# First MLP: two quarters of the up-projection in seven block products each pair of tiles

## The chip, the core and the metric

The program runs on one core of a Trainium2 chip. The metric is the device time of the whole program in microseconds, the median of several executions. The engines in the rows below are TensorE (PE, with its weight loads as PEld), VectorE (DVE), ScalarE (ACT), GpSimd (POOL) and SyncE (SP), which issues the loads of weights.

## What is computed

Two transformer blocks over 512 tokens of width 1024, all in fp32. The first block has an attention mixer, a recurrence, and the MLP that the change is about. The second has two layers whose norms are modulated by `m`, a product of a vector with `ada_w`; the first layer also reads 256 context tokens.

```
hn = rmsnorm(h, norm2_g)
a = square(relu(hn @ w_ff1))        # 1024 -> 4096
h = h + a @ w_ff2                   # 4096 -> 1024
...
m_lat = silu(c) @ ada_w[i] + ada_b[i]       # 6 x 1024 columns for each of two layers
m_ctx = silu(c_ctx) @ ada_w[i] + ada_b[i]
h_lat = rmsnorm(x, g) * (1 + sc_m) + sh_m ; h_ctx = likewise from ctx
```

## The kernel before

Every fp32 operand is held as a pair, a rounded part `hi` and the rest `lo`, and each product of two 128-blocks is three matmuls (`mm3`, L181 to L190: hi.hi, hi.lo, lo.hi). Activations stand transposed, eight tiles of 128 x 512 tokens. A weight tile of 128 x 1024 comes in one load of 512 KB on SP's queue into one of three buffers `wr` (L154); ACT casts it to `wh` (L139), DVE subtracts to `wl` (L128), and 8 x 3 matmuls of 512 columns use the two. `wh` and `wl` have three buffers each. The scheduler fixes the order on each engine before the run; every engine takes its instructions in that order.

The columns of the modulation `m` are computed on DVE beside the MLPs: `ada` (L455) loads a 128 x 1024 tile into a `wr` buffer, the same three as the weights use (L462), and one DVE operation `adaj` multiplies it with silu(c) and sums it (L468). The first 16 columns of layer 0 are needed for the context too and are multiplied twice, with silu(c_ctx) from a second `silu` tile. The table `ADA[0]` says at which step of the first MLP each of the 48 columns is issued. A step is one up-projection tile or one down-projection tile: `tick` in `mlp` (L550) calls `extra` (L710), which looks the step up, and also takes the next piece of the context's work (`CTX`).

The first MLP (`mlp_one`, called at L730) takes the up-projection in four quarters of eight tiles (`ff1`) and the down-projection in four (`ff2`): ff1(0), ff1(1), ff2(0), ff1(2), ff2(1), ff1(3), ff2(2), and the last down-projection in `down` (L317). In all four quarters each tile is multiplied plainly: 24 matmuls of 512 columns.

The MLPs of the second block (`modulated_mlp`, L1108) already use another form. There, from the second quarter on, two weight tiles r0 and r1 are multiplied together, as a 2 x 2 block matrix, with seven products instead of eight (`seven`, L505): DVE forms four sums of weight blocks, seven factors are split, 84 matmuls of 256 columns follow, and DVE recombines the products into two result tiles. The sums of the activations that this needs are made once (`block_sums`, L480). Such groups (p0 to p3) stand between the down-projection columns of the quarter before (m0 to m7) by the lists `MIXED` (L52).

Of the kernel before, what the change touches and what calls it, by code (L numbers as in the profile page):

```python
# [19 lines left out]
F32R = mybir.dt.float32r  # L20
# [4 lines left out]
AF = mybir.ActivationFunctionType  # L25
ALU = mybir.AluOpType
# [4 lines left out]
TC = 256  # L31
# [13 lines left out]
"""  # L45
TAGS = dict(sb=6, hg=16, gate=7)
LATER = (15, 32, 14, 26, 7, 26, 8, 29, 8, 40, 10, 31, 14, 40, 5, 29)
ADA = ((2, 2, 3, 4, 5, 6, 8, 8, 9, 9, 10, 11, 12, 13, 14, 15, 18, 19, 20, 21, 22, 23, 25, 26, 27, 28, 29, 30, 31, 32, 33, 34, 36, 37, 38, 39, 40, 41, 42, 43, 44, 45, 46, 47, 48, 50, 51, 51), (9, 11, 13, 15, 17, 19, 21, 23, 25, 27, 29, 31, 33, 35, 37, 39, 41, 43, 45, 47, 49, 51, 53, 55))
# [31 lines left out]
MAN = ""  # L80
TAIL = "t0 t1 t2 p0 p1 p2 w3"
ENG = dict(scale="P", kr="DP", kp="DP", pt="D", v="D", k="D", cos="P")
CTX = (20, 22, 25, 26, 27, 28, 30)


class Kernel:
# [390 lines left out]

    def block_sums(self, xs, eng=None):  # L480


        B = [[] for _ in range(7)]
        a0, a1 = HALF
        add, sub = ALU.add, ALU.subtract

        def step(k):
            x, y = (self.S(name="bx") for _ in range(2))
            for z, (h, l) in ((x, xs[k]), (y, xs[k + 4])):
                self.tt(z, h.bitcast(F32), l.bitcast(F32), add, eng)  # L490
            out = [(self.F(TC, F32R, "bh", "cb"), self.F(TC, F32R, "bl", "cb")) for _ in range(3)]
            out.append(tuple(z[:, a1] for z in xs[k]))
            t, u = (self.S(name="bt") for _ in range(2))
            t1, t2, t3, t4 = t[:, a0], t[:, a1], u[:, a0], u[:, a1]
            for i, (d, p, q) in enumerate(((t1, x[:, a1], x[:, a0]), (t2, y[:, a1], t1), (t3, y[:, a1], x[:, a1]))):
                self.tt(d, p, q, sub, eng)
                self.split_into(*out[i], d)
            self.tt(t4, y[:, a0], t2, sub, eng)
            for i, b in enumerate((tuple(z[:, a0] for z in xs[k]), tuple(z[:, a0] for z in xs[k + 4]),
                                   tuple(z[:, a1] for z in xs[k + 4]), out[3], *out[:3])):  # L500
                B[i].append(b)
            return lambda: self.split_into(*out[3], t4)
        return B, step

    def seven(self, w, w_next, B, eng):  # L505

        nc = self.nc
        r0, r1 = self.wraw(w), self.wraw(w_next)
# [1 line left out]
        a11, a12, a21, a22 = r0[:, lo], r0[:, hi], r1[:, lo], r1[:, hi]  # L510
        add, sub = ALU.add, ALU.subtract
        a0, a1 = HALF
        s3, s1, s2, s4 = (self.S(name="ws") for _ in range(4))

        def pair(*parts):
            h, l = (self.wp.tile([128, 1024], F32R, tag=t, name=t) for t in ("wh", "wl"))
            for i, p in enumerate(parts):
                c = slice(512 * i, 512 * i + 512)
                self.split_into(h[:, c], l[:, c], p)
            return [self.wsplit((h[:, 512 * i:512 * i + 512], l[:, 512 * i:512 * i + 512]), 4) for i in range(len(parts))]  # L520
        self.tt(s3, a11, a21, sub, eng)
        self.tt(s1, a21, a22, add, eng)
        self.tt(s2, s1, a11, sub, eng)
        self.tt(s4, a12, s2, sub, eng)
        y, x = self.O(), self.P()
        w11, w3 = pair(a11, s3)
        w1, w2 = pair(s1, s2)
        w12, w22 = pair(a12, a22)
        w4, = pair(s4)
        p, s, v = self.H("p1"), self.S(name="p57"), self.H("u2")  # L530
        u = [self.S(name="u") for _ in range(2)]
        k = dict(skip_group_check=True)
        self.mm3(x[:, a0], w11, B[0], True, True)
        nc.scalar.copy(p, x[:, a0])
# [12 lines left out]
        self.tt(u[0][:, a1], y[:, a0], v, add)  # L547
        return u

    def mlp(self, w1, w2, xs, residual, scale=None, extra=None, down=None, begin=None, fast=None):  # L550


        step = [0]
# [43 lines left out]

        def ff1_fast(g, j, r):

            u = self.seven(w1[g * 8 + j], w1[g * 8 + j + 4], B, fast)  # L600
            for i in (1, 0):
                self.stt(u[i], u[i], 0.0, u[i], ALU.max, ALU.mult)
                r[j + 4 * i] = self.split(u[i], tag="f")
                tick()

        if fast:
            B, sums = self.block_sums(xs)
            late = []
            acts = ff1(0, lambda j: late.append(sums(j - 3)) if 3 <= j < 7 else None)
            for f in late:  # L610
                f()
            for g in range(3):
# [53 lines left out]
    def mlp_one(self):  # L666
# [949 lines left out]
```

## Time and profile before

| | us |
|---|---|
| median of 3 executions | 2096.09 |
| lowest and highest | 2095.75, 2098.06 |
| the profiled execution | 2098.49 |
| its span in the trace | 2096.8 |
| first MLP in the trace | 433 to 785 |
| attention of the second block, about | 790 to 1110 |
| second MLP, mixed quarters, about | 1190 to 1400 |

The trace is of one execution. Busy times are those of an engine's records; matmuls overlap one another, so their rate is read from the starts of neighbouring records, not from their lengths. In a row of a timeline the bracket at the end tells how long the engine was idle before it and which instruction ended that.

### The profile page before, as it was taken

Reading aid. Unit: us, or ns where it says so; the run is one execution under the profiler, and the core shown is the slowest. Engines: PE = TensorE matmul, PEld = TensorE weight load, DVE = VectorE, ACT = ScalarE, POOL = GpSimd, SP = SyncE. Lnnn points to the kernel's source line nnn. Section 1 sums busy time; section 2 is a strip of 40 time slices with the busy share of each in tenths; the row PEclk is TensorE's granted clock in tenths of the full one; section 3 lists DMA queues with packets and bytes.
Section 4 is the critical chain, followed back from the end, with each engine's and each line's share of the span. In section 5 each row is a group of like instructions: output and inputs, shape, how many; then the busy total and the mean of one; then the engine's idle time right before and its main releaser. Section 6 shows DMA issues by size and latency. Waiting matters only on the chain.

```text
span 2096.8 us, 29863 instructions
## 1 busy us (share of the span) xinstructions
PE 2057.1 (98%) x11414; PEld 1783.7 (85%) x11414; DVE 1506.5 (72%) x2860; ACT 929.2 (44%) x1600; POOL 218.2 (10%) x234
## 2 busy tenths in 40 slices
PE   9999999999999999899989999999999999999999
PEld 7888888887888888789878888988888889899897
DVE  6868775789766557888868787886457657777673
ACT  5546573444332324567655434443323334444341
POOL 0313220000100001345421000000000001000000
PEclk9999999999999999999999999999999999999999
DMA  5212121556666532101031344443325561232232
GB/s 174 71 61 66 46 85 51 156 180 199 187 186 191 170 121 87 34 22 36 31 121 60 126 155 143 141 161 120 101 89 182 162 192 58 84 109 101 91 111 91
DMA packets 73921, 238.84 MB, mean 114 GB/s; under 512 B 8241, under 2 KB 12593, under 8 KB 73778
## 3 DMA queue, kind: packets, MB, share of 16 engines
q1 hardware_dynamic: 73778, 236.94, 35.5%
q8 instruction: 89, 1.46, 0.3%
q14 instruction: 54, 0.44, 0.1%
HBM read 232.70 MB, written 4.20 MB: 113 GB/s over the span
## 4 chain that ended last, share of the span: by engine, by line
PE 81%; DVE 10%; DMA 3%; ACT 3%; issue 2%; POOL 0%; SPq 0%; POOLq 0%; ACTq 0%; DVEq 0%
PE pq L189 34%; PE ps L189 25%; PE po L189 11%; PE pg L189 2%; DVE wl L128 2%; DMA ada<-in_ada 2%; PE sc L220 1%; PE pl L220 1%; DMA wr<-in_ff 1%; DVE adaj L468 1%; DVE lo L128 1%; ACT wh L139 1%; DVE mod L131 1%; ACT pr L134 1%; PE o L189 1%
## 5 line engine op out<-in xcount | busy, mean ns | idle before, releaser
L139 ACT CAST wh<-wr 128x1024 fp32r<-128x1024 f32 (+3 forms) x362 | 324.8, 907 | 590.6 <-PE pq L189 259.7
L128 DVE TENSOR_TENSOR wl<-wr,wh 128x1024 fp32r<-128x1024 f32 (+3 forms) x362 | 378.4, 1052 | 83.5 <-ACT wh L139 79.7
L189 PE MATMUL pq<-hi,wl 128*128 128x512 f32 (+1 forms) x896 | 342.4, 383 | 0.4 <-DVE wl L128 0.4
L189 PE MATMUL pq<-hi,wh 128*128 128x512 f32 (+1 forms) x896 | 342.1, 383 | 0.0
L189 PE MATMUL pq<-lo,wh 128*128 128x512 f32 (+1 forms) x896 | 342.1, 383 | 0.0
L468 DVE SCALAR_TENSOR_TENSOR adaj<-ada,silu 128x1024 bf16<-128x1024 f32 x112 | 136.8, 1221 | 118.8 <-DMA ada<-in_ada 118.4
L189 PE MATMUL ps<-hi,wh 128*128 128x512 f32 x528 | 208.8, 396 | 2.0 <-ACT hi L139 1.2
L189 PE MATMUL ps<-hi,wl 128*128 128x512 f32 x528 | 209.0, 396 | 0.7 <-DVE wl L128 0.7
L189 PE MATMUL ps<-lo,wh 128*128 128x512 f32 x528 | 207.7, 394 | 0.0
L189 PEld LDWEIGHTS pq<-hi,wl 128*128 128x128 f32 x896 | 168.5, 188 | 33.5 <-DVE wl L128 1.1
L189 PEld LDWEIGHTS pq<-hi,wh 128*128 128x128 f32 x896 | 168.7, 188 | 32.4 <-issue 0.2
L189 PEld LDWEIGHTS pq<-lo,wh 128*128 128x128 f32 x896 | 168.6, 188 | 31.4
L189 PE MATMUL ps<-hl,wh 128*128 128x256 f32 (+1 forms) x752 | 180.3, 330 | 1.7 <-DVE m L128 0.9
L128 POOL TENSOR_TENSOR hl<-mod,hl 128x256 fp32r<-128x256 f32 x36 | 31.7, 890 | 1155.4 <-ACT hl L393 930.2
L189 PEld LDWEIGHTS ps<-hl,wh 128*128 128x128 f32 x752 | 128.0, 190 | 16.5 <-DVE u L128 2.0
L189 PE MATMUL ps<-hl,wl 128*128 128x256 f32 (+1 forms) x376 | 123.8, 329 | 0.0
L189 PEld LDWEIGHTS ps<-hi,wh 128*128 128x128 f32 x528 | 99.3, 188 | 23.7 <-ACT hi L139 1.4
L189 PEld LDWEIGHTS ps<-hi,wl 128*128 128x128 f32 x528 | 99.5, 188 | 22.7 <-DVE wl L128 1.6
L131 DVE SCALAR_TENSOR_TENSOR x<-pq,m,x 128x512 f32<-128x512 f32 (+1 forms) x88 | 60.4, 686 | 79.8 <-PE pq L189 79.7
L189 PEld LDWEIGHTS ps<-lo,wh 128*128 128x128 f32 x528 | 99.7, 189 | 20.0 <-DVE lo L128 0.4
L189 PE MATMUL po<-hl,wh 128*128 128x256 f32 (+1 forms) x528 | 115.4, 312 | 0.0
L139 ACT CAST wh<-ws 128x512 fp32r<-128x512 f32 x96 | 56.8, 619 | 96.1 <-PE po L189 66.7
(407 smaller groups left out, 4519.6 us busy)
## 6 DMA issues: line engine op xcount, KB each, us to landing
wr<-in_f SPq DMA_DIRECT2D x128, 512.0 KB, 3.5
ada<-in_ada SPq DMA_DIRECT2D x96, 512.0 KB, 3.9
wr<-in_ff SPq DMA_DIRECT2D x64, 512.0 KB, 4.2
wr<-in_w_in SPq DMA_DIRECT2D x41, 512.0 KB, 3.6
wr<-in_gw_v SPq DMA_DIRECT2D x16, 512.0 KB, 3.4
wr<-in_gw_u SPq DMA_DIRECT2D x16, 512.0 KB, 3.5
wr<-in_gw_o SPq DMA_DIRECT2D x16, 512.0 KB, 4.3
wr<-in_w_out SPq DMA_DIRECT2D x8, 512.0 KB, 3.7
```

The source lines that it names most:

```text
L128: return (eng or self.nc.vector).tensor_tensor(out=out, in0=a, in1=b, op=op)
L131: (eng or self.nc.vector).scalar_tensor_tensor(out=out, in0=a, scalar=s, in1=b, op0=op0, op1=op1)
L134: self.nc.scalar.activation(out=out, in_=x, func=func, scale=scale, bias=bias, **k)
L139: nc.scalar.copy(hi, x)
L189: self.nc.tensor.matmul(out, l, r, start=start and i == j == 0, stop=stop and i == n - 1 and j == 2, **k)
L220: self.nc.tensor.matmul(out, l, r, start=start, stop=stop)
L468: nc.vector.scalar_tensor_tensor(out=d, in0=w, scalar=1.0, in1=s, op0=ALU.mult, op1=ALU.mult, accum_out=m[:, n:n + 1])
```

## The change

The third and fourth quarter of the first MLP's up-projection go through `seven`, as in the MLPs of the second block. `mlp` gets two parameters. `plain=2` keeps quarters one and two plain; then the first down-projection runs, with `block_sums` issued behind its columns m4 to m7, and two mixed groups follow, by `MIXED[0]` and `MIXED[1]`. `tags` puts the 24 tiles of the sums into the buffers in which the context lay (`cx`, `xc`). The weight sums of a group go into a `silu` tile, two at a time, where s2 and s4 overwrite s3 and s1; the results go into `relu` tiles. Since this MLP scales its rows by rstd, DVE now forms relu times scale and ACT squares it.

The table of the modulation columns is new: the first 16 are issued at steps 2 to 14, none at steps 15 to 23, and the other 32 from step 24 to 54, one behind every step. The context's work goes from steps 20 to 30 to steps 8 to 20. In `seven` the sums and splits stand in another order, for all callers.

```diff
@@ tables
-ADA = ((2, 2, 3, 4, 5, 6, 8, 8, 9, 9, 10, 11, 12, 13, 14, 15, 18, 19, 20, 21, 22, 23, 25, 26, ...
+ADA = ((2, 2, 3, 3, 4, 5, 6, 7, 8, 8, 9, 10, 11, 12, 13, 14, 24, 24, 25, 26, 27, 28, 29, 30, ...
-CTX = (20, 22, 25, 26, 27, 28, 30)
+CTX = (8, 15, 16, 17, 18, 19, 20)
@@ block_sums
-            out = [(self.F(TC, F32R, "bh", "cb"), self.F(TC, F32R, "bl", "cb")) for _ in range(3)]
+            out = [tuple(self.F(TC, F32R, "b", next(tags) if tags else "cb") for _ in range(2)) for _ in range(3)]
...
-            t, u = (self.S(name="bt") for _ in range(2))
+            t, u = self.two(tags, "bt")
@@ new, called by block_sums and seven
+    def two(self, small, name):
+        if not small:
+            return [self.S(name=name) for _ in range(2)]
+        t = self.F(1024, name=name, tag="silu")
+        return t[:, :512], t[:, 512:]
@@ seven
-        s3, s1, s2, s4 = (self.S(name="ws") for _ in range(4))
...
+        s3, s1 = self.two(small, "ws")
+        s2, s4 = (s3, s1) if small else self.two(small, "ws")
...
         self.tt(s3, a11, a21, sub, eng)
         self.tt(s1, a21, a22, add, eng)
+        hl = pair()
+        w11, w3 = part(hl, 0, a11), part(hl, 1, s3)
         self.tt(s2, s1, a11, sub, eng)
+        hl = pair()
+        w1 = part(hl, 0, s1)
         self.tt(s4, a12, s2, sub, eng)
+        w2 = part(hl, 1, s2)
+        hl = pair()
+        w12, w22 = part(hl, 0, a12), part(hl, 1, a22)
+        w4 = part(pair(), 0, s4)
         y, x = self.O(), self.P()
-        w11, w3 = pair(a11, s3)
-        w1, w2 = pair(s1, s2)
-        w12, w22 = pair(a12, a22)
-        w4, = pair(s4)
         p, s, v = self.H("p1"), self.S(name="p57"), self.H("u2")
-        u = [self.S(name="u") for _ in range(2)]
+        u = [self.F(name="u", tag="relu") if small else self.S(name="u") for _ in range(2)]
@@ ff1_fast
             for i in (1, 0):
-                self.stt(u[i], u[i], 0.0, u[i], ALU.max, ALU.mult)
+                self.stt(u[i], u[i], 0.0, u[i] if scale is None else scale, ALU.max, ALU.mult)
+                if scale is not None:
+                    self.act(u[i], u[i], AF.Square)
                 r[j + 4 * i] = self.split(u[i], tag="f")
                 tick()
@@ mlp
-            B, sums = self.block_sums(xs)
+            B, sums = self.block_sums(xs, tags=tags)
             late = []
-            acts = ff1(0, lambda j: late.append(sums(j - 3)) if 3 <= j < 7 else None)
+            if plain == 1:
+                acts = ff1(0, lambda j: late.append(sums(j - 3)) if 3 <= j < 7 else None)
+            else:
+                acts = ff1(0)
+                nx = ff1(1)
+                for m in range(8):
+                    ff2(0, acts, (m,))
+                    if m >= 4:
+                        late.append(sums(m - 4))
+                acts = nx
             for f in late:
                 f()
-            for g in range(3):
+            for g in range(plain - 1, 3):
                 nx = [None] * 8
-                for what in (MIXED[0] if g == 0 else MIXED[1]).split():
+                for what in (MIXED[0] if g == plain - 1 else MIXED[1]).split():
@@ mlp_one
-        self.mlp(a["ff1"], a["ff2"], xs, residual, r2, extra, (self.Sum(self, gains=g2), done), begin=(2, start))
+        self.mlp(a["ff1"], a["ff2"], xs, residual, r2, extra, (self.Sum(self, gains=g2), done), (2, start),
+                 nc.vector, 2, iter(["cx"] * 8 + ["xc"] * 16))
```

`MIXED[0]` is "m0 m1 m2 p0 m3 p1 m4 p2 m5 p3 m6 m7", `MIXED[1]` is "m0 m1 p0 m2 p1 m3 m4 p2 m5 p3 m6 m7".

DVE, in the kernel before, third quarter: the first tile's relu (`relu`), its split (`lo`), a modulation column (`adaj` and its bias `m`), and the split of a later weight tile (`wl`).

```order
L131 SCALAR_TENSOR_TENSOR relu_6046<-ps_6021,rstd_4064 128x512 [waits PE_49]
L128 TENSOR_TENSOR wl_6147<-wr_6144,wh_6146 128x1024 [waits DMAHW2_49,Activation_49]
L468 SCALAR_TENSOR_TENSOR adaj_6227,m_79<-ada_6225,silu_4065 128x1024 [waits DMAHW5_49]
L128 TENSOR_TENSOR lo_6050<-relu_6046,hi_6049 128x512 [waits Activation_49]
L128 TENSOR_TENSOR m_79<-m_79,cols_72 128x1 [waits DVE_49]
L131 SCALAR_TENSOR_TENSOR relu_6089<-po_6064,rstd_4064 128x512 [waits PE_49]
```

DVE, in the changed kernel, where the first seven-product group of the third quarter begins: `h` takes up the result of the down-projection column m2, `b`, `bt` and `lo` belong to the block sums, `ws` are the weight sums, and `wl` 5571, 5578, 5585 and 5591 the splits of the group's factors.

```order
L128 TENSOR_TENSOR h_3813<-h_3813,pq_5532 128x512 [waits PE_49]
L128 TENSOR_TENSOR b_5423<-bt_5428,b_5422 128x256 [waits Activation_49]
L128 TENSOR_TENSOR bt_5428<-bx_5419,bt_5428 128x256 [waits DVE_49]
L128 TENSOR_TENSOR b_5425<-bt_5428,b_5424 128x256 [waits Activation_49]
L128 TENSOR_TENSOR b_5427<-bt_5428,b_5426 128x256 [waits Activation_49]
L128 TENSOR_TENSOR lo_3883<-bt_5428,hi_3882 128x256 [waits Activation_49]
L128 TENSOR_TENSOR ws_5567<-wr_5563,wr_5565 128x512 [waits DMAHW0_49,DVE_49]
L128 TENSOR_TENSOR ws_5567<-wr_5565 128x512
L128 TENSOR_TENSOR wl_5571<-ws_5567,wh_5570 128x512 [waits Activation_49]
L128 TENSOR_TENSOR wl_5578<-ws_5567,wh_5577 128x512 [waits Activation_49]
L128 TENSOR_TENSOR ws_5567<-ws_5567,wr_5563 128x512 [waits DVE_49]
L128 TENSOR_TENSOR wl_5585<-wr_5563,wh_5584 128x512 [waits Activation_49]
```

The weight sums and splits of the group stand behind the addition of m2's result and five operations of the block sums.

PE, in the kernel before, the same place: the first matmuls of the third quarter's first tile.

```order
L189 MATMUL ps_6021<-hi_3760,wh_6017 128x512 [waits Activation_49]
L189 MATMUL ps_6021<-lo_3761,wh_6017 128x512
L189 MATMUL ps_6021<-hi_3760,wl_6018 128x512 [waits DVE_49]
L189 MATMUL ps_6021<-hi_3800,wh_6017 128x512
L189 MATMUL ps_6021<-lo_3801,wh_6017 128x512
```

PE, in the changed kernel, first group of the third quarter: the last two matmuls of the first product (into `ps`, with the factor a11), and the beginning of the second (into `po`, whose factor is the weight sum s3).

```order
L189 MATMUL ps_5595<-lo_3883,wh_5570 128x256
L189 MATMUL ps_5595<-hi_3882,wl_5571 128x256
L189 MATMUL po_5594<-b_5267,wh_5570 128x256 [waits Activation_49]
L189 MATMUL po_5594<-b_5268,wh_5570 128x256
L189 MATMUL po_5594<-b_5267,wl_5571 128x256 [waits DVE_49]
L189 MATMUL po_5594<-b_5320,wh_5570 128x256
L189 MATMUL po_5594<-b_5321,wh_5570 128x256
```

The second product needs the `hi` part of s3 from ACT and its `wl` from DVE; the first product is 12 matmuls of 256 columns, so that the wait for the second factor stands 12 short matmuls behind the column m2.

SP, in the kernel before, third quarter: weight tiles and modulation columns take turns.

```order
L157 DMA wr_6187<-in_ff1 128x1024 [waits DMAHW0_49,DVE_49]
L462 DMA ada_6225<-in_ada 128x1024 [waits DMAHW3_49,DVE_49]
L157 DMA wr_6230<-in_ff1 128x1024 [waits DMAHW2_49,DVE_49]
L462 DMA ada_6268<-in_ada 128x1024 [waits DMAHW5_49,DVE_49]
L157 DMA wr_6273<-in_ff1 128x1024 [waits DMAHW4_49,DVE_49]
L462 DMA ada_6311<-in_ada 128x1024 [waits DMAHW7_49,DVE_49]
```

SP, in the changed kernel, in the first mixed group: two `wr` of `in_ff1` are r0 and r1 of a group of seven products, the single `wr` of `in_ff2` a down-projection column.

```order
L157 DMA wr_5752<-in_ff1 128x1024 [waits DMAHW7_49,DVE_49]
L157 DMA wr_5754<-in_ff1 128x1024 [waits DMAHW4_49,DVE_49]
L462 DMA ada_5888<-in_ada 128x1024 [waits DMAHW3_49,DVE_49]
L462 DMA ada_5899<-in_ada 128x1024 [waits DMAHW7_49,DVE_49]
L157 DMA wr_5904<-in_ff2 128x1024 [waits DMAHW0_49,DVE_49]
L462 DMA ada_5936<-in_ada 128x1024 [waits DMAHW6_49,DVE_49]
L157 DMA wr_5941<-in_ff1 128x1024 [waits DMAHW5_49,DVE_49]
L157 DMA wr_5943<-in_ff1 128x1024 [waits DMAHW1_49,DVE_49]
L462 DMA ada_6077<-in_ada 128x1024 [waits DMAHW2_49,DVE_49]
L462 DMA ada_6088<-in_ada 128x1024 [waits DMAHW5_49,DVE_49]
```

Six loads now belong to one group and one down-projection column, in the order r0, r1, column, column, m, column.

## Rows read from the trace of the kernel before

**Rows 1.** The page, part 1: busy us, share of the span, instructions.

```profile
PE 2057.1 (98%) x11414; PEld 1783.7 (85%) x11414; DVE 1506.5 (72%) x2860; ACT 929.2 (44%) x1600; POOL 218.2 (10%) x234
```

**Rows 2.** The page, part 4: the chain that ended last, by engine.

```profile
PE 81%; DVE 10%; DMA 3%; ACT 3%; issue 2%; POOL 0%; SPq 0%; POOLq 0%; ACTq 0%; DVEq 0%
```

**Rows 3.** Windows: us, busy us per engine (instructions), clock, DMA share, GB/s.

```profile
432.58:524.85 92.27, 90.61 (x400) 73.48 (x399) 85.36 (x172) 40.84 (x61) 0.00 (x0) 1.00 0.61 193
...
569.00:710.00 141.00, 140.56 (x656) 117.53 (x655) 91.74 (x159) 50.63 (x69) 3.10 (x2) 1.00 0.61 187
790.00:1110.00 320.00, 295.80 (x1965) 265.31 (x1964) 255.16 (x661) 190.69 (x422) 108.87 (x68) 0.98 0.17 55
1190.00:1400.00 210.00, 207.94 (x1321) 188.49 (x1320) 175.15 (x308) 86.15 (x145) 0.00 (x0) 1.00 0.45 147
...
860.00:867.00 7.00, 6.42 (x26) 5.08 (x24) 6.94 (x15) 3.29 (x7) 1.92 (x2) 0.54 0.01 4
```

**Rows 4.** Timeline of PE, first MLP, 512 columns: start us, length us, instruction.

```profile
700.12 0.39 PE L189 MATMUL ps<-hi,wh 128*128 128x512 f32 x1
700.35 0.39 PE L189 MATMUL ps<-lo,wh 128*128 128x512 f32 x1
```

**Rows 5.** Timeline of PE, last MLP, 256 columns.

```profile
1816.35 0.28 PE L189 MATMUL po<-bh,wh 128*128 128x256 f32 x1
1816.47 0.28 PE L189 MATMUL po<-bl,wh 128*128 128x256 f32 x1
```

**Rows 6.** Waits of PE, 432.58 to 524.85: us in total, times, longest.

```profile
PE po L189 <- DVE wl L128: 0.8, 2, 0.5
PE ps L189 <- DVE wl L128: 0.5, 1, 0.5
```

**Rows 7.** Waits of PE, second MLP, 1190 to 1400.

```profile
PE ps L189 <- DVE m L128: 0.9, 1, 0.9
PE ps L189 <- DVE u L128: 0.7, 1, 0.7
PE pq L189 <- DVE wl L128: 0.4, 1, 0.4
```

**Rows 8.** Timeline of DVE in the second MLP.

```profile
1302.49 1.22 DVE L468 SCALAR_TENSOR_TENSOR adaj<-ada,silu 128x1024 bf16<-128x1024 f32 x1 [1.89 <-DMA ada<-in_ada]
...
1304.43 0.42 DVE L128 TENSOR_TENSOR u<-u,u 128x256 f32<-128x256 f32 x1
1304.77 1.22 DVE L128 TENSOR_TENSOR wl<-wr,wh 128x1024 fp32r<-128x1024 f32 x1
1305.91 0.42 DVE L128 TENSOR_TENSOR u<-po,u 128x256 f32<-128x256 f32 x1
...
1307.91 0.69 DVE L131 SCALAR_TENSOR_TENSOR u<-u 128x512 f32<-128x512 f32 x1
1308.51 0.69 DVE L128 TENSOR_TENSOR ws<-wr 128x512 f32<-128x512 f32 x1
...
1311.52 1.22 DVE L468 SCALAR_TENSOR_TENSOR adaj<-ada,silu 128x1024 bf16<-128x1024 f32 x1
1312.66 0.08 DVE L468 DVE_READ_ACCUMULATOR adaj<-ada,silu 128x1 f32 x1
```

**Rows 9.** Timeline of SP's issues in the second MLP.

```profile
1298.92 0.33 SPq L462 DMA_DIRECT2D ada<-in_ada  x1
```

**Rows 10.** DMA issues, 432 to 790: count, KB each, median us to landing.

```profile
wr<-in_ff SPq DMA_DIRECT2D x61, 512.0 KB, 4.2
ada<-in_ada SPq DMA_DIRECT2D x46, 512.0 KB, 4.1
```

**Rows 11.** Waits of DVE, second MLP, 1190 to 1400.

```profile
DVE ws L128 <- DMA wr<-in_f: 11.6, 9, 2.2
DVE adaj L468 <- DMA ada<-in_ada: 9.5, 6, 3.8
```

**Rows 12.** Timeline of PE in the second MLP.

```profile
1304.45 0.50 PE L189 MATMUL ps<-hl,wh 128*128 128x256 f32 x2 [0.86 <-DVE m L128]
```

More of the change, by code (lines that the diff above doesn't have):

```diff
@@ L47 @@
 LATER = (15, 32, 14, 26, 7, 26, 8, 29, 8, 40, 10, 31, 14, 40, 5, 29)
-ADA = ((2, 2, 3, 4, 5, 6, 8, 8, 9, 9, 10, 11, 12, 13, 14, 15, 18, 19, 20, 21, 22, 23, 25, 26, 27, 28, 29, 30, 31, 32, 33, 34, 36, 37, 38, 39, 40, 41, 42, 43, 44, 45, 46, 47, 48, 50, 51, 51), (9, 11, 13, 15, 17, 19, 21, 23, 25, 27, 29, 31, 33, 35, 37, 39, 41, 43, 45, 47, 49, 51, 53, 55))
+ADA = ((2, 2, 3, 3, 4, 5, 6, 7, 8, 8, 9, 10, 11, 12, 13, 14, 24, 24, 25, 26, 27, 28, 29, 30, 31, 32, 33, 34, 35, 36, 37, 38, 39, 40, 41, 42, 43, 44, 45, 46, 47, 48, 49, 50, 51, 52, 53, 54), (9, 11, 13, 15, 17, 19, 21, 23, 25, 27, 29, 31, 33, 35, 37, 39, 41, 43, 45, 47, 49, 51, 53, 55))
 WARM = 9
@@ L475, in ada, with block_sums @@
             self.tt(self.m[2][:, lo:h], self.m[2][:, lo:h], self.cols[:, c + lo:c + h], ALU.add)
-    def block_sums(self, xs, eng=None):
+    def block_sums(self, xs, eng=None, tags=None):
         B = [[] for _ in range(7)]
@@ L503, in block_sums, with seven @@
         return B, step
-    def seven(self, w, w_next, B, eng):
+    def two(self, small, name):
[3 more added lines that the diff above has]
+        return t[:, :512], t[:, 512:]
+    def seven(self, w, w_next, B, eng, small=None):
         nc = self.nc
@@ L512, in seven, with pair, part @@
         a0, a1 = HALF
-        s3, s1, s2, s4 = (self.S(name="ws") for _ in range(4))
[L515 to L520, printed above, removed]
+        s3, s1 = self.two(small, "ws")
+        s2, s4 = (s3, s1) if small else self.two(small, "ws")
+        def pair():
+            return [self.wp.tile([128, 1024], F32R, tag=t, name=t) for t in ("wh", "wl")]
+        def part(hl, i, p):
+            c = slice(512 * i, 512 * i + 512)
+            self.split_into(hl[0][:, c], hl[1][:, c], p)
+            return self.wsplit((hl[0][:, c], hl[1][:, c]), 4)
         self.tt(s3, a11, a21, sub, eng)
         self.tt(s1, a21, a22, add, eng)
+        hl = pair()
+        w11, w3 = part(hl, 0, a11), part(hl, 1, s3)
         self.tt(s2, s1, a11, sub, eng)
+        hl = pair()
+        w1 = part(hl, 0, s1)
         self.tt(s4, a12, s2, sub, eng)
+        w2 = part(hl, 1, s2)
+        hl = pair()
+        w12, w22 = part(hl, 0, a12), part(hl, 1, a22)
+        w4 = part(pair(), 0, s4)
         y, x = self.O(), self.P()
-        w11, w3 = pair(a11, s3)
-        w1, w2 = pair(s1, s2)
-        w12, w22 = pair(a12, a22)
-        w4, = pair(s4)
         p, s, v = self.H("p1"), self.S(name="p57"), self.H("u2")
-        u = [self.S(name="u") for _ in range(2)]
+        u = [self.F(name="u", tag="relu") if small else self.S(name="u") for _ in range(2)]
         k = dict(skip_group_check=True)
@@ L548, in seven, with mlp @@
         return u
-    def mlp(self, w1, w2, xs, residual, scale=None, extra=None, down=None, begin=None, fast=None):
+    def mlp(self, w1, w2, xs, residual, scale=None, extra=None, down=None, begin=None, fast=None, plain=1, tags=None):
         step = [0]
@@ L598, in ff1_fast @@
         def ff1_fast(g, j, r):
-            u = self.seven(w1[g * 8 + j], w1[g * 8 + j + 4], B, fast)
+            u = self.seven(w1[g * 8 + j], w1[g * 8 + j + 4], B, fast, tags)
             for i in (1, 0):
-                self.stt(u[i], u[i], 0.0, u[i], ALU.max, ALU.mult)
+                self.stt(u[i], u[i], 0.0, u[i] if scale is None else scale, ALU.max, ALU.mult)
+                if scale is not None:
+                    self.act(u[i], u[i], AF.Square)
                 r[j + 4 * i] = self.split(u[i], tag="f")
```

## The prediction

> **What bounds the kernel now.** I read the busy totals first: TensorE (PE) is busy 2057.1 of 2096.8 us [rows 1], and 81% of the chain that ended last is PE [rows 2]. So a microsecond of PE work taken away is a microsecond gained, unless PE then waits. Next came the table of windows [rows 3]. In the first MLP the plain stretch keeps PE full (90.61 of 92.27 us, 140.56 of 141 us) while VectorE (DVE) is busy 85.36 and 91.74 us. The second MLP, 1190 to 1400 us, is the one whose up-projection already goes in seven products with loads of modulation columns in between: PE 207.94 of 210 us, DVE 175.15, DMA 147 GB/s. It is the nearest relative of what is to come. Its waits of PE [rows 7] are three, 2.0 us in all, each for a DVE result. To the start-to-start pitch of the matmuls PE lost 3.2 us there, in four places, over 11 groups of seven products, 0.29 us each; the first MLP lost 5.0 us over all its length (433 to 785), most of it in the first two quarters (the largest waits: [rows 6]).
>
> **The matmuls: minus 6.4 us.** Two plain weight tiles of the up-projection cost 48 matmuls of 512 columns, which start 0.23 us apart ([rows 4]; over 24 in a row 5.44 us, 0.2267 each): 10.88 us. The seven products of the same tiles cost 84 of 256 columns, which start 0.12 us apart [rows 5]: 10.08 us. That is 0.80 us for a pair, and quarters three and four have eight pairs: 6.4 us. [...]
>
> **What the products cost on DVE.** Durations are taken start to start [rows 8]: 0.60 us for 512 columns (1307.91 to 1308.51), 0.34 for 256 (1304.43 to 1304.77), 1.14 for a 1024-column split and for a modulation column (1304.77 to 1305.91, 1311.52 to 1312.66), 0.07 for its bias. A group of seven products (p) has 4 sums of weights, 7 splits, 5 recombinations of half width, 2 relu-times-scale and 2 splits of the result: 15 x 0.60 + 5 x 0.34 = 10.7 us. A down-projection column (m) has its split and an addition, 1.75 us; a modulation column 1.22 us. The new table puts one modulation column behind every step from 24 on, and an interval of one p and one m has three steps: 10.7 + 1.75 + 3 x 1.22 = 16.1 us of DVE against 10.08 + 5.44 = 15.52 us of PE. Over both mixed groups (8 p, 16 m, 32 columns) DVE has 153 us beside PE's 168. That is 91%, where the second MLP has 83% [rows 3]. ACT has slack: the square moves there, and stays well under PE.
>
> [...]
>
> **The loads.** An interval loads six tiles of 512 KB (two for p, one for m, three columns) through the three `wr` buffers: 6 x 0.524 MB in 15.52 us is 203 GB/s, where the stage now runs at 187 to 193 [rows 3]. More than the rate, the order counts. By the SyncE (SP) order quoted above, r0 and r1 of a p hold two buffers until their last split, so two columns and m follow one another through the third: each goes out when the one before has been read, and a load that is waited for takes 3.57 us (issue 1298.92 [rows 9], use 1302.49 [rows 8]); the median here is 4.2 [rows 10]. Three times (3.57 + 1.2) is 14.3 us of 15.52, before any queueing behind other work on DVE, which takes its instructions in order: a column that isn't there holds up the split behind it. The second MLP shows this in small, 11.6 us of DVE idle for weights and 9.5 for columns in 210 us [rows 11], and the wait of PE for `m` at 1304.45 [rows 12] is such a chain: the column of 1302.49 came 1.89 us late, and the recombinations and a split behind it too.
>
> **The walk.** I followed the changed order by hand with these durations, an instruction starting when its engine, its inputs and its buffer are free. At the first p, PE comes from m2 and runs its first product, 12 x 0.12 = 1.4 us, then wants the split of the second factor. On DVE the addition of m2's result (0.6, which cannot start before PE ends m2) and five block-sum operations (1.7) stand ahead of the two weight sums (1.2) and that split (0.7): 4.2 us and a little for the signals, so PE waits 2.9 us. The modulation column behind it gets its buffer late and puts 0.85 on m3. p1 loses 0.15; at p2 and p3 the planner starts the product with a22 ahead of the rest of the s2 product, before DVE has its split (1 to 1.4), and m's weights come a microsecond late: 2.4 and 1.9. Together 8.2 us in the first mixed group. The second has no block sums and shorter backlogs: 1.2, 1.0, 0.4, 0.2, together 2.8. Sum 11 us. Bounds: at the second MLP's loss per p, 8 x 0.29 = 2.3 us; with all loads at 4.2 us instead of 3.57, 13 to 15, and up to 20 if the backlog never clears. I take 11, since the walk uses this order and the walked interval (16.1 against 15.52) lies beyond what the second MLP has (one or two columns: 13.7 to 15).
>
> **What else moves.** The 24 block-sum tiles, some 15.7 us of DVE (4 x (2 x 0.60 + 8 x 0.34)), lie under the first down-projection, where the new table asks for no column (steps 15 to 23) and PE runs 43 us of plain work: nothing, but for the five left over that the walk has counted. If that cover were gone they would cost up to the 15.7. The context steps go to the same place: nothing. The first two quarters keep their 16 double columns, two of them earlier: plus or minus 1 to 2 us around the 4 us lost there now. [...] The later MLPs change only in the order of DVE inside `seven`: plus or minus 1.
>
> **The sum.** 2098.49 - 6.4 + 11 = 2103.1 us against the profiled execution (its span 2096.8 and 1.7 around it). That execution is 2.4 us above the median of the three, so the forecast for the median is 2096.09 - 6.4 + 11 = 2100.7 us.
>
> **The rivals.** 0.2% is about what a measurement of this kernel can tell from no change, 4.2 us: 2091.9 and 2100.3 are the borders.
>
> First rival, not slower: DVE's slack of 15 us over the two groups is used well, since the plan lets m's and p's work run ahead, and PE loses no more than in the second MLP, 2.3 to 4 us. Its price is those losses, its place the eight p, and it decides if the columns are read within an interval, that is, if the load chain stays under 15.5 us. For it: the second MLP does this with 83% of DVE and loses little. Against: three columns an interval, not one or two, and the block sums ahead of p0. Time 2096.09 - 6.4 + 2.3 to 4 = 2092 to 2094; with the plus or minus of the other stages 2089 to 2095, centre 2092.
>
> Second rival, slower by more: the loads take 4.2 us or more throughout, the third buffer's chain becomes 3 x (4.2 + 1.2) = 16.2 us and, with what queues behind it on DVE, sets the interval; eight intervals lose 2 to 2.5 us each, 15 to 20 us, or the 2.9 us wait at p0 brings the low clock as in [rows 3]. Time 2105 to 2110. For it: the median of 4.2 us and 203 GB/s asked. Against: those 4.2 us include loads issued while others were under way that nobody waited for. [...]
>
> [...] That the change doesn't do what it says is excluded: the order shows 84 matmuls of 256 columns in place of 48 for each pair.
>
> **How the numbers follow.** The forecast (losses of 8 to 14 us, 2097.7 to 2103.7) 0.45, of which 0.24 lies above 2100.3 and 0.21 within; the first rival 0.20, half faster, half within; the second 0.20, all slower; the third 0.15, of which 0.03 faster, 0.09 within, 0.03 slower. Faster 0.10 + 0.03 = 0.13; within 0.21 + 0.10 + 0.09 = 0.40; slower 0.24 + 0.20 + 0.03 = 0.47. The range leaves out a tenth on each side: 2091.5 (half of the first rival is above) to 2108. The forecast's own range is 2097.7 to 2103.7.
>
> **What would show it.** In the profile after: eight p whose matmuls start 0.12 us apart (minus 6.4); a wait of PE of 2 to 3 us for a DVE `wl` at the first p; waits for `wl` of 1 to 2.5 us at p2 and p3 of the first mixed group, smaller ones in the second; DVE some 91% busy over the two groups, with idle for `ada` and `wr`. I am wrong if PE's losses in the mixed groups are under 5 us (first rival), or over 14 (second), or if the stage between 790 and 1110 us changes its length by more than 3 us.

## The result and the profile after

The changed kernel takes 2109.23 us (median; 2107.09 to 2111.58), the kernel before 2096.74 in the same series: ratio 1.0058, 95% interval 1.0046 to 1.0069, so 12.5 us slower. The forecast was 2100.7, slower by 4.6: the sign was right, the size was not, and the time lies just above the range's end of 2108. Some 8 us are to be explained.

The profiled execution of the changed kernel took 2107.09 us, with a span of 2105.4. The page's busy totals and the chain that ended last:

```profile
PE 2053.9 (98%) x11702; PEld 1793.1 (85%) x11702; DVE 1569.9 (75%) x3012; ACT 959.3 (46%) x1680; POOL 214.3 (10%) x234
...
PE 74%; DVE 14%; DMA 5%; ACT 3%; issue 2%; POOL 0%; SPq 0%; POOLq 0%; ACTq 0%; DVEq 0%
```

Beside [rows 1] and [rows 2]: PE is busy 3.2 us less, DVE 63 us more (the weight sums, more splits, the block sums: 8 x 6 + 15.7 = 64 by the prediction's costs), and the chain passes through DVE for 14% of the span where it was 10%, through DMA for 5% where it was 3%.

To place the loss I compared the starts of corresponding matmuls. From the first matmul of the first MLP to one of its last (786.07 us before, 800.74 after) the changed kernel takes 15.0 us more. The attention stage then takes 5.4 us less in these two executions, and all after it 0.7 less. Then I summed, over each part of the MLP, what the starts of PE's matmuls lie further apart than 0.2267 us (512 columns) or 0.120 us (256 columns). I call this the loss of that part. Before, it was 4.0 us in the first two quarters and 1.7 in the rest. After, it is 6.1 in the first two quarters, 0.8 in the first down-projection, **9.8 in the first mixed group and 10.3 in the second**. That closes: 21.3 us more loss (27.0 against 5.7) minus 6.4 for the products gives 14.9. Between these two executions the whole differs by 8.6 us (2107.09 against 2098.49), between the medians by 12.5.

Windows of the changed kernel, columns as in [rows 3]: the first two quarters, most of each of the two mixed groups (they run from about 580 to 674 and from 674 to 768), and the stretches behind the two longest waits.

```profile
432.58:525.00 92.42, 89.91 (x391) 73.11 (x390) 87.37 (x183) 40.76 (x61) 0.00 (x0) 0.98 0.65 198
...
596.00:680.00 84.00, 78.11 (x487) 70.29 (x486) 76.32 (x145) 40.86 (x69) 0.00 (x0) 0.98 0.55 181
680.00:760.00 80.00, 73.15 (x467) 66.26 (x467) 66.17 (x124) 33.81 (x58) 0.00 (x0) 0.98 0.53 166
```

```profile
600.90:605.90 5.00, 4.73 (x25) 4.52 (x26) 4.81 (x8) 2.90 (x5) 0.00 (x0) 0.68 0.17 31
695.20:698.00 2.80, 2.80 (x13) 2.80 (x14) 1.89 (x4) 0.17 (x1) 0.00 (x0) 0.50 0.75 211
```

In the first group DVE is busy 76.32 of 84 us, the 91% of the prediction. In the second it is 83%, less than the prediction asked for: there DVE itself waits. Its waits for the loads of columns, 580 to 674 and then 674 to 768 us (us in total, times, longest):

```profile
DVE adaj L468 <- DMA ada<-in_ada: 2.2, 4, 0.8
DVE adaj L468 <- DMA ada<-in_ada: 7.0, 6, 2.8
```

The two groups differ, and one place of each shows how.

**First group.** Timeline of PE at the first seven products (start, length, instruction, the idle time before it and what ended it):

```profile
597.75 0.28 PE L189 MATMUL ps<-hi,wl 128*128 128x256 f32 x1
600.95 0.50 PE L189 MATMUL po<-b,wh 128*128 128x256 f32 x2 [2.92 <-ACT wh L139]
601.67 0.39 PE L189 MATMUL po<-b,wl 128*128 128x256 f32 x1 [0.22 <-DVE wl L128]
...
604.47 0.63 PE L189 MATMUL po<-b,wh 128*128 128x256 f32 x2
604.89 0.41 PE L189 MATMUL po<-b,wl 128*128 128x256 f32 x1
605.11 0.63 PE L189 MATMUL po<-b,wh 128*128 128x256 f32 x2
```

DVE in the same time:

```profile
597.16 0.68 DVE L128 TENSOR_TENSOR h<-h,pq 128x512 f32<-128x512 f32 x1
597.76 0.42 DVE L128 TENSOR_TENSOR b<-bt,b 128x256 fp32r<-128x256 f32 x1
598.10 0.42 DVE L128 TENSOR_TENSOR bt<-bx,bt 128x256 f32<-128x256 f32 x1
598.43 0.76 DVE L128 TENSOR_TENSOR b<-bt,b 128x256 fp32r<-128x256 f32 x2
599.10 0.42 DVE L128 TENSOR_TENSOR lo<-bt,hi 128x256 fp32r<-128x256 f32 x1
599.55 1.29 DVE L128 TENSOR_TENSOR ws<-wr 128x512 f32<-128x512 f32 x2
600.93 1.35 DVE L128 TENSOR_TENSOR wl<-ws,wh 128x512 fp32r<-128x512 f32 x2
```

This is the walk, row for row: the addition of m2's result, five operations of the block sums, two weight sums, then the split. PE waits 2.92 us where 2.9 was forecast. What the walk left out stands in the window above: the granted clock is 0.68 over the next 5 us. From 602.97 on three matmuls take 0.64 us (604.47 to 605.11) instead of 0.36, for 2.8 us; that is 1.2 us more. At the group's other products PE waits less, and for other things than the walk had, DVE's recombinations (`u`) and a copy on ACT (`p`). From 580 to 674:

```profile
PE ps L189 <- DVE u L128: 2.0, 3, 1.0
PE po L189 <- ACT p L549: 0.8, 2, 0.4
```

**Second group.** DVE, and then PE, at its first seven products:

```profile
689.63 0.68 DVE L128 TENSOR_TENSOR wl<-ws,wh 128x512 fp32r<-128x512 f32 x1
693.12 1.23 DVE L468 SCALAR_TENSOR_TENSOR adaj<-ada,silu 128x1024 bf16<-128x1024 f32 x1 [2.81 <-DMA ada<-in_ada]
...
694.27 0.42 DVE L128 TENSOR_TENSOR u<-p 128x256 f32<-128x256 f32 x1
694.61 0.41 DVE L128 TENSOR_TENSOR u<-ps,p 128x256 f32<-128x256 f32 x1
```

```profile
695.08 0.58 PE L189 MATMUL ps<-hi,wh 128*128 128x256 f32 x1 [3.13 <-DVE u L128]
```

DVE has nothing to do but stands 2.81 us before a modulation column whose load was issued at 689.13, when a buffer had come free. Behind it in DVE's order wait the recombinations (`u`), one of which reads `ps`, and PE's next matmul into `ps` waits for a `u`. So PE stands 3.13 us for a load that has nothing to do with it, and then runs 2.6 us at a granted clock of 0.50 (1.2 us more). This place has nearly half of the second group's loss.

### The profile page after: what moved, and what is told of

Read it like the earlier page. It is cut to its first block, busy times and chain, and to the rows that moved or that the text cites. A ratio compares the mean times of both kernels' runs of the same rounds, so it can differ in the third digit from the quotient of the medians.

```text
span 2105.4 us, 30672 instructions
## 1 busy us (share of the span) xinstructions
PE 2053.9 (98%) x11702; PEld 1793.1 (85%) x11702; DVE 1569.9 (75%) x3012; ACT 959.3 (46%) x1680; POOL 214.3 (10%) x234
## 4 chain that ended last, share of the span: by engine, by line
PE 74%; DVE 14%; DMA 5%; ACT 3%; issue 2%; POOL 0%; SPq 0%; POOLq 0%; ACTq 0%; DVEq 0%
PE pq L189 29%; PE ps L189 25%; PE po L189 9%; DVE wl L128 3%; DMA ada<-in_ada 3%; PE pg L189 2%; DVE adaj L468 2%; DMA wr<-in_ff 2%; PE sc L220 1%; DVE lo L128 1%; PE pl L220 1%; ACT wh L139 1%; ACT pr L134 1%; DVE mod L131 1%; DVE ws L128 1%
## 5 line engine op out<-in xcount | busy, mean ns | idle before, releaser
L189 PE MATMUL ps<-hi,wh 128*128 128x512 f32 (+1 forms) x528 | 203.3, 386 | 8.8 <-DVE u L128 5.4
L189 PE MATMUL ps<-hi,wl 128*128 128x512 f32 (+1 forms) x528 | 202.7, 384 | 1.6 <-DVE wl L128 1.4
L189 PE MATMUL ps<-lo,wh 128*128 128x512 f32 (+1 forms) x528 | 201.5, 382 | 0.0
L139 ACT CAST wh<-ws 128x512 fp32r<-128x512 f32 x128 | 76.6, 620 | 129.0 <-PE po L189 79.1
L189 PEld LDWEIGHTS ps<-hi,wl 128*128 128x128 f32 x528 | 100.3, 190 | 21.3 <-DVE wl L128 2.9
```

What stands on the lines that cost most here:

```text
L139: nc.scalar.copy(hi, x)
L189: self.nc.tensor.matmul(out, l, r, start=start and i == j == 0, stop=stop and i == n - 1 and j == 2, **k)
```

## The experiments

Two theories of the loss stood against each other: A, the 32 loads of columns in the mixed quarters come late and hold up DVE; B, it is the amount of DVE work. A third, C, blamed the tables, the block sums or the products themselves. The table has each kernel's median minus that of the kernel before in its series, the ratio's interval, the lengthening of the first MLP in the trace, and the losses of its parts in us (the parts as above).

| kernel | median | ratio, 95% | first MLP | quarters 1, 2 | down 1 | group 1 | group 2 |
|---|---|---|---|---|---|---|---|
| the change | +12.5 | 1.0046 to 1.0069 | +15.0 | 6.1 | 0.8 | 9.8 | 10.3 |
| tables alone | +0.4 | 0.9996 to 1.0014 | +1.3 | | | | |
| no loads | +14.5 | 1.0059 to 1.0092 | +18.5 | 6.0 | 16.6 | 7.1 | 0.8 |
| no columns | -0.6 | 0.9989 to 1.0008 | -1.7 | 8.0 | 0.8 | 0.5 | 0.9 |
| sums early | +13.8 | 1.0052 to 1.0082 | +10.8 | 5.7 | 0.9 | 9.3 | 6.9 |
| work, no loads | +10.9 | 1.0033 to 1.0066 | +11.4 | 5.8 | 0.8 | 15.0 | 1.8 |
| loads, no work | +4.3 | 1.0015 to 1.0033 | +5.3 | 5.8 | 0.8 | 3.8 | 6.8 |
| columns spread | +20.1 | 1.0082 to 1.0112 | +12.4 | 2.7 | 7.2 | 9.5 | 5.1 |
| spread, sums early | +14.0 | 1.0051 to 1.0081 | +4.6 | 4.7 | 8.6 | 1.2 | 2.1 |
| 8 in the last down | +5.4 | 1.0017 to 1.0040 | +1.4 | 3.4 | 2.8 | 3.9 | 2.8 |
| fourth quarter, 8 in the last down | +2.6 | 1.0002 to 1.0020 | -3.2 | | | | |
| fourth quarter, 8 in the group | +0.6 | 0.9997 to 1.0017 | +3.8 | | | | |

**The tables alone**, in the kernel before:

```diff
-ADA = ((2, 2, 3, 4, 5, 6, 8, 8, 9, 9, 10, ...
+ADA = ((2, 2, 3, 3, 4, 5, 6, 7, 8, 8, 9, ...
-CTX = (20, 22, 25, 26, 27, 28, 30)
+CTX = (8, 15, 16, 17, 18, 19, 20)
```

> The kernel before with the change's two tables alone (when the 48 modulation columns and the context's work are issued); all four quarters stay plain. In the changed kernel the first MLP ends 15.0 us later than before, 2.1 of which were lost in the first two quarters, where PE waited 1.6 and 1.1 us near 456 us. Theory A (the columns' loads hold up DVE in the mixed quarters): plain work has enough cover, so only those 2 us appear, 2097 to 2100 us. Theory C (the tables are bad for any work): the first MLP gets 6 us or more longer, 2103 us or more.

2097.85 us, no difference to be measured. Beside plain quarters a column at every step costs nothing that can be measured in the whole. C falls for the tables.

**No loads**: the columns from 16 on are multiplied from a tile already in memory.

```diff
+            if layer == 0 and n >= 16:
+                w = self.sc[0]
+            else:
...
```

> The changed kernel in which the modulation columns from 16 on are multiplied from a tile that already lies in memory, so their values are wrong: their 32 loads of 512 KB are left out, their DVE work stays. Theory A (DVE stands behind columns whose load is late, and the loads take turns on one buffer): the waits in the mixed quarters fall from 18 to about 7 us (5 at the first group with the block sums, 2 elsewhere), time 2097 to 2099. Theory B (it is the amount of DVE work, 16.1 us an interval beside 15.5 of PE): the waits stay at 15 us or more, time 2106 to 2109.

2111.97 us, which looked like B. The trace says otherwise: nothing is left of the loss in the second group (0.8), but 16.6 us appeared before the mixed groups. The longest waits of PE from 525 to 570 us (us in total, times, longest):

```profile
PE ps L189 <- DVE hl L131: 4.8, 1, 4.8
PE ps L189 <- ACT hl L134: 3.6, 1, 3.6
PE pq L189 <- DVE wl L128: 1.6, 1, 1.6
```

With no load to wait for, the planner put the 32 multiplications earlier on DVE, the first some 60 places, the last some 240 (the expectation below, written for the next runs, says 130), among the context's work. The run changed two things and tells the theories apart only in the second group.

**No columns**: neither loaded nor multiplied.

```diff
+            if layer == 0 and n >= 16:
+                continue
             w = self.wp.tile([128, 1024], F32, tag="wr", name="ada")
```

> The changed kernel without the modulation columns from 16 on: neither loaded nor multiplied (a constant stands in their place). Theory A: close to the run without their loads alone, 1 to 2 us lower for the shorter queue at the first group, 2095 to 2098. Theory B: this run alone recovers the loss, by 10 us or more against the run without loads. Both say that the first MLP is then no longer than before.

2096.82 us, and the mixed groups lose 0.5 and 0.9 us: seven products beside plain down-projection columns run without waits here, block sums and all. The 6.4 us are there. Against the run without loads it recovers 15 us, as B wanted, but that run was spoilt; against C it decides: all of the mixed groups' loss comes with the columns. Its first two quarters lose 8.0 us, twice as much as before, so the whole gains nothing.

**Block sums earlier**:

```diff
-                    if m >= 4:
-                        late.append(sums(m - 4))
+                    if m < 4:
+                        late.append(sums(m))
```

> The changed kernel with the four pieces of the block sums issued behind columns m0 to m3 of the first down-projection instead of m4 to m7. My walk puts 2.9 us of PE's wait at the first seven-product group down to five operations of the sums that stand ahead of the weights' splits; in the trace that wait is 3.1 us and brings the granted clock to 0.5 for some matmuls after it, 5.2 us together. If so, this run gains 4 to 5 us, 2104 to 2106. If the wait is the loads' (theory A for this place too), the group's first split comes no earlier: 2108 to 2110.

2111.22 us. In the trace the first MLP is 4 us shorter than the change's, which the attention stage takes back. The wait at the first group's first products is gone from the trace, and still that group loses 9.3 us: 0.6 to 2.0 us at a place, over all its products. It is another loss than before. In the change 30 of the 40 operations of the sums start after 580 us, where the group begins; here all are done by then, and DVE is not behind: from 580 to 674 it waits for columns

```profile
DVE adaj L468 <- DMA ada<-in_ada: 7.0, 8, 2.1
```

where that was 2.2 us in the change. At the longest wait of PE there a late column stands ahead of the recombination that PE needs (DVE's row, then PE's):

```profile
657.88 1.22 DVE L468 SCALAR_TENSOR_TENSOR adaj<-ada,silu 128x1024 bf16<-128x1024 f32 x1 [2.07 <-DMA ada<-in_ada]
659.84 0.38 PE L189 MATMUL po<-hi,wh 128*128 128x256 f32 x1 [1.80 <-DVE u L128]
```

With the sums out of the way the first group looks like the second. What I expected of the whole, a gain of 4 to 5 us, did not come.

**The two halves.** So that the order nearly stays, the column is multiplied from the weight tile loaded last (work, no loads), or the load stays and only 16 of the tile's 1024 elements are multiplied (loads, no work).

```diff
+            if layer == 0 and n >= 16:
+                w = self.last_raw
+            else:
...
```

> The changed kernel in which each modulation column from 16 on is multiplied from the weight tile loaded last instead of from a tile of its own (its value is wrong): the DVE work stays where it is in the order, the 32 loads and their turns on the three buffers are gone. The run without loads could not tell this, since there the planner moved the columns up to 130 places earlier on DVE and the loss with them (15 us near 540 us). Theory A (late loads): waits in the mixed quarters fall from 18 to 7 us or less, 2098 to 2101. Theory B (amount of DVE work): they stay at 14 or more, 2106 to 2110.

```diff
                 d = self.F(1024, BF16, "adaj", "adaj")
+                if layer == 0 and n >= 16:
+                    d, w, s = d[:, :16], w[:, :16], s[:, :16]
```

> The opposite half: the 32 loads stay, with their buffers and waits, but each column from 16 on is multiplied over 16 of its 1024 elements alone (wrong values), so 1.1 us of DVE work less for each. Theory A: the waits stay at 14 us or more, 2106 to 2110. Theory B: they fall to 7 or less, 2098 to 2101. If each theory holds half, both runs end near 2103.

2108.55 and 2101.90 us, so by the time B is the larger half. The windows show more. Each pair of rows has most of the first group, then of the second, at the same times though the groups shift by some us; first without columns, then the work alone, then the loads alone:

```profile
596.00:680.00 84.00, 83.88 (x538) 76.32 (x537) 61.88 (x101) 39.07 (x67) 0.00 (x0) 1.00 0.29 95
680.00:760.00 80.00, 79.85 (x500) 71.83 (x499) 57.15 (x91) 38.62 (x63) 0.00 (x0) 1.00 0.36 119
```

```profile
596.00:680.00 84.00, 75.12 (x464) 68.02 (x463) 75.07 (x141) 38.61 (x67) 0.00 (x0) 0.94 0.29 94
680.00:760.00 80.00, 79.11 (x504) 71.64 (x504) 70.92 (x133) 37.19 (x63) 0.00 (x0) 1.00 0.29 95
```

```profile
596.00:680.00 84.00, 82.01 (x514) 73.24 (x513) 61.89 (x141) 38.33 (x66) 0.00 (x0) 1.00 0.57 184
680.00:760.00 80.00, 75.96 (x483) 68.81 (x482) 57.23 (x125) 36.34 (x61) 0.00 (x0) 0.98 0.56 181
```

In the first group the work alone takes PE down to 75.12 of 84 us (loss 15.0) and the loads alone hardly (3.8). In the second it is the other way round: DVE busy 70.92 of 80 us and PE hardly waits (1.8), while the loads with DVE at 57.23 cost 6.8. So the second group is lost to late loads in DVE's order, and the run without loads says the same (0.8).

The first group's 15.0 are not DVE's work by itself. Some 5.8 of them lie at the first products, where DVE comes late out of the block sums, 3.61 us in the wait itself. Another 6.2 lie at one place, where DVE stands before a weight tile, with the recombination behind it in its order, and PE waits 3.13 us (in the first window above, 596 to 680, the granted clock is 0.94, against 1.00 without columns and with the loads alone):

```profile
611.00 1.29 DVE L128 TENSOR_TENSOR ws<-wr 128x512 f32<-128x512 f32 x2 [2.56 <-DMA wr<-in_ff]
613.83 0.58 PE L190 MATMUL ps<-hi,wh 128*128 128x256 f32 x1 [3.13 <-DVE u L128]
```

That tile's load was issued at 606.06, when DVE, late from the sums, had read the buffer out. So in the first group DVE's work with the sums ahead of it costs PE directly, and a second time through weights that are issued late. This run's columns also read the weight buffers and stand 2 to 18 places (one 35) earlier on DVE than in the change; what that adds is not shown. The two losses don't add up: 16.8 and 10.6 apart, 20.1 together.

**Columns spread**: the first 16 at their old steps, 8 at the first down-projection, one an interval in the mixed groups, 8 in the second MLP; and the same with the sums early.

```diff
+ADA = ((2, 2, 3, 4, 5, 6, 8, 8, 9, 9, 10, 11, 12, 13, 14, 15, 16, 17, 18, 19, 20, 21, 22, 23, 24, 25, 26, 29, 32, 35, 38, 39, 40, 41, 44, 47, 48, 51, 54, 55, 99, ...
...
                     self.ada(1, n, n + 1)
+            if layer == 0 and 1 <= i <= 8:
+                self.ada(0, 39 + i, 40 + i)
```

> The changed kernel with its modulation columns spread otherwise: the first 16 at their old steps, 8 at the eight steps of the first down-projection, 16 in the mixed quarters (one at each down-projection column, so one an interval instead of three), 8 in the first quarter of the second MLP. DVE then has 10.7 + 1.75 + 1.2 = 13.7 us an interval beside 15.5 of PE, four loads instead of six, as the second MLP, which loses 0.29 us a group. Theories A and B alike: waits in the mixed quarters 2 to 5 us, first two quarters as before, 2092 to 2096. If the block sums or the seven products themselves are to blame (theory C), the waits stay over 10 us, 2100 or more.

> The run before with the block sums behind columns m0 to m3 of the first down-projection instead of m4 to m7. Without columns in the mixed quarters the wait at the first group was gone even with the sums late; so I expect no more than 1 to 2 us from the sums here, 2091 to 2095. If the sums hold the first group up by themselves, as my walk had it, 3 to 5 us below the run before.

2117.73 and 2111.62 us, both far off what I expected. The mixed groups did what was expected in the second of the two (1.2 and 2.1 us), so one column an interval can be borne, if nothing else is late: the first of the two has as many and loses 9.5 and 5.1. Half of the 9.5 is the wait at the first products (4.81 us), now with all of the block sums between the group's start and it; with the sums early this wait is gone:

```profile
607.31 0.79 PE L189 MATMUL po<-b,wh 128*128 128x256 f32 x2 [4.81 <-ACT wh L139]
```

But the rest of the work went where it costs: the first down-projection loses 7.2 and 8.6 us. With the sums early DVE is full there (47.82 us busy from 526 to 580); with the sums late it is not (36.56), and stands 6.8 us before columns. And some of the columns meant for the second MLP (3 and 4 of the 8 by 1130 us) were taken up by the planner at the end of the attention stage, which takes 5 to 6.5 us longer. In the second run one of them stands on DVE before its load. The second fence has PE's largest wait from 1040 to 1130 us (in total),

```profile
1111.68 1.23 DVE L468 SCALAR_TENSOR_TENSOR adaj<-ada,silu 128x1024 bf16<-128x1024 f32 x1 [2.50 <-DMA ada<-in_ada]
```

```profile
PE po L220 <- DVE sq L128: 4.9, 2, 4.1
```

where the kernel before has 1.4 us and multiplies no column.

**Eight columns in the last down-projection**, 24 in the mixed groups, the sums early:

```diff
             x = residual(m, ps, slice(0, T))
             sums.add(x, m)
+            if self.hook:
+                self.hook()
```

> The changed kernel with the first 16 columns at their old steps, no column in the first down-projection, 24 instead of 32 in the mixed quarters (one or two an interval), 8 behind the first four columns of the last down-projection, where DVE is half idle; the block sums behind m0 to m3. DVE over a mixed group: 4 x 10.7 + 8 x 1.75 + 12 x 1.22 = 71.4 us beside PE's 83.8, 85%, as in the second MLP. If the loss is DVE work and loads together, as the two halves say, the mixed groups lose 4 to 6 us instead of 20, the first quarters 4 as before: 2094 to 2098. If one or two columns an interval still cost most of it, 2102 or more.

2103.05 us. The mixed groups lose 6.7 us, about what they save. The first down-projection lost 2.8, and the columns in the last one delay the attention stage, whose first sum of squares now waits; no run without columns there has this wait:

```profile
792.18 1.05 PE L220 MATMUL po<-sel,sq 128*128 128x2 f32 x8 [2.44 <-DVE sq L128]
```

**The fourth quarter alone**, with the columns at plain steps and eight in the last down-projection, or eight in the mixed group:

```diff
-                 nc.vector, 2, iter(["cx"] * 8 + ["xc"] * 16))
+                 nc.vector, 3, iter(["cx"] * 8 + ["xc"] * 16))
```

> Seven products in the fourth quarter alone: three quarters plain, block sums behind m0 to m3 of the second down-projection, 22 columns beside plain steps (at before's pace), 2 at the first two steps of the mixed group and 8 in the last down-projection; the context's work at its old steps. The gain is then 4 x 0.80 = 3.2 us, and a mixed group without columns lost 0.5 to 2 us in the other runs: 2094.5 to 2097. If the seven products cost the first MLP more than they save even so, 2098 or more.

> The run with the fourth quarter alone in seven products, but without columns in the last down-projection, where they made the attention stage begin 2 us late: 24 columns stand beside plain steps at nearly before's pace, 8 in the mixed group, at its down-projection columns (one an interval). The products save 3.2 us; a mixed group with one column an interval should lose 1 to 2.5 us (DVE 13.7 beside 15.5 of PE): first MLP 1 to 2 us shorter, 2095 to 2097. If already one column an interval costs as much as the products save, 2097.5 or more.

2100.27 and 2098.66 us. The first has the first MLP 3.2 us shorter, the whole saving of four pairs, and gives part of it back behind: PE waits 1.62 us, until 788.45, for a sum of squares, and by 796 us 1.9 of the 3.2 are gone. The rest, up to the 2.6 us of the median, I can't place in one trace. The second is no different from the kernel before: with one column an interval its mixed group loses some 5.8 us, more than it saves, 3.3 of it at one place. DVE there, and the matmul that waits (`ws` is the sum of the next products' weights, the 1024-column `wl` the split that PE wants):

```profile
689.62 0.43 DVE L128 TENSOR_TENSOR u<-ps,p 128x256 f32<-128x256 f32 x1 [0.33 <-PE ps L189]
693.39 1.29 DVE L128 TENSOR_TENSOR ws<-wr 128x512 f32<-128x512 f32 x2 [3.34 <-DMA wr<-in_ff]
694.60 0.42 DVE L128 TENSOR_TENSOR u<-u,u 128x256 f32<-128x256 f32 x1
694.94 1.22 DVE L128 TENSOR_TENSOR wl<-wr,wh 128x1024 fp32r<-128x1024 f32 x1
696.21 0.50 PE L189 MATMUL pq<-hi,wl 128*128 128x512 f32 x1 [3.28 <-DVE wl L128]
```

It is the picture of the second group again, now with a weight tile that is late. No kernel that I ran beats the kernel before.

## Why the prediction was wrong

**The matmuls, minus 6.4: right.** Without columns the mixed groups lose 1.4 us over eight pairs, and with the fourth quarter alone the first MLP is 3.2 us shorter, 0.80 a pair.

**DVE's work: right in the first group.** It is 91% busy there, as worked out for both. Over both windows it is 142.5 of 164 us, 87%: the stretch got longer, and in the second group DVE waits.

**The walk: near for the first group, wrong for the second. This is the step that failed.** "The second has no block sums and shorter backlogs: 1.2, 1.0, 0.4, 0.2, together 2.8": it lost 10.3. There DVE is less behind, so it stands before loads that have not come, 7.0 us before six of its 14 columns and 4.4 before four weight tiles, and everything in its order waits. I had described this under the loads ("a column that isn't there holds up the split behind it") and then priced the second group by DVE's backlog, with each load at 3.57 us. The halves show it: there the loads alone cost 6.8 and the work alone 1.8. By the prediction's own signs it is wrong twice: the mixed groups lost 20.1 us, where over 14 meant the second rival, and the attention stage changed by more than 3 us.

The first group's 8.2 were 9.8. Its first wait came as walked, 2.92 us for 2.9. The rest agrees in its sum by luck: 1.2 us are the clock; the 0.85 on m3 did not come; and at p2 and p3, which lost 1.7 and 1.4 us for 2.4 and 1.9, PE waited for recombinations and a copy, not for a `wl`.

**The clock: priced in a rival, not in the sum.** Behind two waits of about 3 us the granted clock was 0.50 (603.00 to 605.70 and 695.20 to 698.00), 1.2 us each, and behind the waits near 456 us it was 0.52 (459.2 to 462.4).

**The first two quarters: 2.1 us, the edge of plus or minus 1 to 2.** PE waits 1.5 and 0.9 us near 456 us, and the clock falls for eight matmuls of 512 columns, which start 0.43 us apart:

```profile
458.99 0.53 PE L189 MATMUL ps<-hi,wl 128*128 128x512 f32 x1 [0.92 <-DVE wl L128]
...
460.17 0.63 PE L189 MATMUL ps<-hi,wl 128*128 128x512 f32 x1
460.59 0.63 PE L189 MATMUL ps<-hi,wh 128*128 128x512 f32 x1
```

The three runs in the table with the old steps for the first 16 columns lost 2.7 to 4.7 there, those with the new steps 5.7 to 8.0.

**The block sums as the cause at the first group: right for the wait, not for the group.** With the sums early the wait is gone, and with one column an interval the group's loss falls from 9.5 to 1.2 us. With three columns an interval the group lost as much elsewhere, in its longest wait to a late column; and without columns the sums cost nothing, though they stand as late. That they "lie under the first down-projection" was wrong: 30 of their 40 operations start after it.

**The rivals.** The second rival's time, 2105 to 2110, is what came, at a chance of 0.20; the first's (2092) needed columns that don't cost. The second's mechanism is half of what came. The loads landed no later than before (median 3.6 us for weights and 4.1 for columns from 570 to 760, [rows 10]); they were issued late: SP's queue waits 177 us from 570 to 770 before issuing, 113 of them, as the trace puts it, for DVE's instructions. And the work without the columns' loads cost more than the loads. The third rival's chance, 0.15, was for a mixed stretch that breaks even; the two groups lost 20.1 us for the 6.4 saved. DVE's 0.60 us for 512 columns, with which the forecast and the rivals reckon, held: the trace of the changed kernel again has the starts 0.60 us apart:

```profile
705.09 0.68 DVE L128 TENSOR_TENSOR wl<-ws,wh 128x512 fp32r<-128x512 f32 x1
705.69 0.68 DVE L128 TENSOR_TENSOR h<-h,pq 128x512 f32<-128x512 f32 x1
```

**What stays open.** The attention stage was 5.4 us shorter in the change's profiled execution than in that of before, more than the 3 us that the prediction allowed, 6.4 shorter with the tables alone, and 5 to 6.5 longer in the spread runs. That allowance, a part also of the first rival's "plus or minus of the other stages", was my estimate, and no run shows it. The plan of that stage differs from kernel to kernel and one trace of each doesn't tell plan from execution; over medians the change gave back 2.5 of its 15.0 us. How the first group's loss divides between DVE's work, the sums and the weights that come late behind them is not settled. A column buffer apart from the weights' three was not tried.

## What to carry to other kernels

The product that saves PE time by giving DVE more work paid here only where DVE kept the room (for 6.4 us saved the mixed groups lost 1.4 without columns and 20.1 with them): count what else is planned onto DVE in the same stretch (here 39 us of columns under 168 us of PE) and run once with that left out, which shows both the saving and its price. DVE took its work in order, and a load that nobody needed soon stopped work that was needed now (2.81 us before a column, 3.13 us of PE behind it), most where DVE was not behind (7.0 us before columns in the second group, 2.2 in the first); price both regimes, the backlog and the wait for the load, for each stretch. And work moved out of a stretch must be followed to where the planner puts it: three of my moves cost more in the next stage than they freed.

## What I had not expected of the hardware

In the changed kernel the granted clock fell to 0.50 behind single waits of PE of 2.92 and 3.13 us in stretches that were otherwise full, for 2.6 to 2.8 us each, and behind two waits of 1.47 and 0.92 us in a row, for 3 us (0.52 from 459.2 to 462.4); in the kernel before it was 0.54 from 860 to 867 [rows 3], behind gaps of 1.05 and 1.61 us in the attention stage. Behind the other waits of 1 to 2 us in the changed kernel's mixed groups, the longest 1.82 us, the pitch stayed at 0.12 us. The length of a wait alone doesn't tell: in the run with the sums early the clock was 0.50 behind the wait of 1.80 us, and in the run with the fourth quarter and eight columns in the group it was 1.00 behind one of 3.28 us. The windows behind these two:

```profile
661.00:664.40 3.40, 3.40 (x12) 2.82 (x11) 3.40 (x6) 1.25 (x2) 0.00 (x0) 0.50 0.74 248
696.20:699.60 3.40, 3.39 (x15) 2.78 (x16) 2.79 (x6) 1.25 (x2) 0.00 (x0) 1.00 0.52 159
```
